# Second matrix of a feed-forward block by seven block products for 18 of 22 inner features, with two of four weight sums made in DRAM

## The chip, the core and the metric

The kernel runs on one core of a Trainium2 chip. The core has five engines that run side by side, each with its own instruction stream in order: TensorE (PE, matmuls; its weight loads are PEld), VectorE (DVE), ScalarE (ACT), GpSimd (POOL) and SyncE (SP, which here only issues DMA transfers). Sixteen DMA engines move data between DRAM and the on-chip memory SBUF; matmuls write into eight banks of PSUM. The metric is the time of one execution in microseconds (us).

## The reference

Two encoder layers over 544 tokens (512 of a first request, 32 of a later one). Each layer is a half-step feed-forward block (FFN), a mixer, and a second FFN, each with a residual and a LayerNorm. All numbers are float32.

```python
# x: 544 x 1024; D_MODEL = 1024, D_FF = 2816, ALPHA = 4 ** 0.25
def swiglu(x, w_in, w_out):
    gate, up = jnp.split(x @ w_in, 2, axis=-1)
    return (jax.nn.silu(gate) * up) @ w_out

x = layer_norm(ALPHA * x + 0.5 * swiglu(x, w_ffn_in[0], w_ffn_out[0]), ln_g[0], ln_b[0])
proj = x @ w_in                    # 1024 x 2560: pooling, convolution, attention inputs
...                                # mix = concat(pool, conv, attn) @ w_out
x = layer_norm(ALPHA * x + mix, ln_g[1], ln_b[1])
x = layer_norm(ALPHA * x + 0.5 * swiglu(x, w_ffn_in[1], w_ffn_out[1]), ln_g[2], ln_b[2])
```

## The kernel before, in words

**Layout.** Activations stand with channels on the 128 partitions and the 544 tokens along the row, in two halves of 272 (`HALF`). A model vector is `NK` = 8 tiles, the hidden vector `NF` = 22 tiles, called features. The residual stream is `y`, a view of `ya`.

**Splitting.** Every factor of a matmul is split into a high part (rounded, written by ACT) and a low part (the difference, by DVE). A product is then three matmuls: high weight by high data, low weight by high data, high weight by low data (`mm_h` L255, `mm_l` L259). A weight of 128x128 with a half of 272 tokens is the standard matmul here.

**Weights.** `Weights` holds a list of units in the order of use. SP loads a unit's raw blocks into the `raw` buffers; `part` makes the high (L172, ACT) and low (L173, DVE) parts in groups of up to 512 columns. A plain unit ("t") is one output column; a unit "s" holds four blocks of weights, from which `sums` makes four sums (L198, DVE) and seven groups. `get` lets the next unit's load and splitting be written one unit ahead of its matmuls, two for plain units.

**FFN.** `plan` walks over the 22 features. The first `NPLAIN` = 3 are computed plainly, the other 19 by seven products of blocks (`seven`, `hidden`): the token halves and the halves of the input channels form a 2x2 scheme, in which seven products replace eight. Their data sums come from `Blocks.add`. Each product goes through one PSUM bank and is taken out by ACT or DVE while the next runs (L341). The finished feature `sg` is split into `hh` and `hl`.

The second matrix runs in parts of `FSPLIT` = 8, 7, 7 features. As soon as one more feature than a part needs is done, each of its 8 output columns is computed plainly and added to `y` by DVE (`resid`, L449 and L451). The last part runs in `out_phase`, together with the LayerNorm.

**LayerNorm in `out_phase`.** After the second column a rough mean is subtracted (`shift`). For each further column DVE subtracts it (L377), ACT squares, and POOL adds to two accumulators (L380, L381); the columns that come last get the subtraction from POOL ahead of time (L388). For the last `nb` columns (2, in the program's last FFN 4) the two token halves run apart: all first halves, then all second halves, and DVE adds them to the accumulators (`add_last`, L393 to L396). `stats` (L405) sums the accumulators over the partitions on PE, `spread` (L419) copies the scale to all partitions, `scale` writes the next stage's data. PE runs remaining tail matmuls between these steps; a scheduler orders the instructions by priority.

Of the kernel before, what the change touches and what calls it, by code (L numbers as in the profile page):

```python
# [10 lines left out]
F32 = mybir.dt.float32  # L11
# [5 lines left out]
P = 128  # L17
# [13 lines left out]
FSPLIT = (8, 7, 7)  # L31
# [4 lines left out]
FB = 5  # L36
W_BUFS = 10
RAW_BUFS = 3
# [35 lines left out]
def encoder_kernel(  # L74
# [6 lines left out]
    w2: bass.AP,  # L81
    wi: bass.AP,
# [19 lines left out]
    xp = ctx.enter_context(tc.tile_pool(name="xp", bufs=34))  # L102
# [54 lines left out]
    class Weights:  # L157
# [24 lines left out]
        def load(self):  # L182
            kind, src, n = self.units[self.loaded]
            self.loaded += 1
            if kind == "t":
                raw = self.fetch()
                c = 0
                for part in src if isinstance(src, tuple) else (src,):
                    w = part.shape[-1]
                    nc.sync.dma_start(out=raw[:, c:c + w], in_=part)  # L190
                    c += w
                self.ready.append(Tile([self.group(raw[:, g:min(g + G, n)]) for g in range(0, n, G)]))
            else:
                self.ready.append(self.sums(src))

        def add(self, a, b):
            r = big["pool"].tile([P, G], F32, tag="sum", name="sum", bufs=4)
            V.tensor_tensor(out=r, in0=a, in1=b, op=ALU.add)  # L198
            return r

        def sums(self, src):

            raws = [self.fetch() for _ in range(2)]
            for i, raw in enumerate(raws):
                nc.sync.dma_start(out=raw, in_=src[:, 2 * i * G:2 * (i + 1) * G])
            b11, b12, b22, b21 = (raw[:, c:c + G] for raw in raws for c in (0, G))
            g11, g21 = self.group(b11), self.group(b21)
            r1 = self.add(b11, b12)
            r2 = self.add(r1, b22)
            g2, g1 = self.group(r2), self.group(r1)  # L210
            g3 = self.group(self.add(b12, b22))
            g22 = self.group(b22)
            return g11, g21, g2, g1, g3, g22, self.group(self.add(r2, b21))

        def first(self, x):

            units = self.units[:NSTART]
            raws = [self.fetch() for _ in units]
            tiles = [[self.new_group() for _ in range(2)] for _ in units]
            n = 2  # L220
            for i in range(NK // n):
                ks, cs = slice(n * i, n * i + n), slice(n * i * P, n * (i + 1) * P)
                nc.scalar.dma_start(out=ya[:, ks, HS[0]], in_=xT[:, ks, HS[0]])
                for raw, (_, src, _) in zip(raws, units):
                    o = slice(cs.start % G, cs.start % G + n * P)
                    nc.sync.dma_start(out=raw[:, cs], in_=src[cs.start // G][:, o])
            for i in range(NK // n):
                cs = slice(n * i * P, n * (i + 1) * P)
                o = slice(cs.start % G, cs.start % G + n * P)
                for k in range(n * i, n * i + n):  # L230
                    split(y[k], x[k], HS[0])
                for raw, groups in zip(raws, tiles):
                    hi, lo = groups[cs.start // G]
                    self.part(raw[:, cs], hi[:, o], lo[:, o])
# [17 lines left out]
    def mm_h(acc, w, x, k, h, first):  # L252

        for i, v in enumerate(w.at(k)):
            PE.matmul(acc[:, :HALF], v, x[k][0][:, HS[h]], start=first and i == 0, stop=False)  # L255

    def mm_l(acc, w, x, k, h, last):

        PE.matmul(acc[:, :HALF], w.at(k)[0], x[k][1][:, HS[h]], start=False, stop=last)  # L259
# [25 lines left out]
    def split(t, x, sl=slice(0, T), eng=None):  # L285
        hh, hl = x
        S.activation(out=hh[:, sl], in_=t[:, sl], func=AF.Copy)
        (eng or V).tensor_tensor(out=hl[:, sl], in0=t[:, sl], in1=hh[:, sl].bitcast(F32), op=ALU.subtract)
# [12 lines left out]
    def new_b(name):  # L301
# [852 lines left out]
```

## Time and profile before

| | |
|---|---|
| time, median of 3 runs | 2003.87 us (2002.77 to 2006.32) |
| profiled execution | 2006.03 us |
| its span | 2004.2 us |
| PE busy | 1973.7 us, 98% |
| DVE busy | 1449.9 us, 72% |
| ACT busy | 993.6 us, 50% |
| POOL busy | 225.6 us, 11% |
| moved on the load queue | 172.07 MB, 27.4% of the engines' time |

The busy shares are means over the whole span; a stage can be far from them. A matmul's printed duration overlaps the next one's, so the price of a matmul is the distance between starts. "Idle before <-releaser" names what ended an engine's idle time; an instruction without it followed the one before at once. The granted clock of PE was 0.99 of full speed.

### The profile page before, as it was taken

How to read it: one execution, taken by the hardware profiler on the slowest of the kernel's cores; microseconds unless marked ns; L12 is line 12 of the kernel's file. 1: busy time of each engine (PE TensorE's matmuls, PEld its weight loads, DVE VectorE, ACT ScalarE, POOL GpSimd, SP SyncE). 2: the span in 40 equal slices, each digit the busy share in tenths (PEclk: the TensorE clock that was granted, in tenths of full speed). 3: DMA queues.
4: the chain of work that ended last, by engine and by line, in shares of the span. 5: the costliest groups of instructions: out<-in, count | busy, mean ns of one | idle time of the engine just before them, and what ended most of it. 6: DMA issues, size and time to landing. Idle time of an engine off the chain costs nothing.

```text
span 2004.2 us, 38173 instructions
## 1 busy us (share of the span) xinstructions
PE 1973.7 (98%) x15446; PEld 1937.3 (97%) x15446; DVE 1449.9 (72%) x2806; ACT 993.6 (50%) x2000; POOL 225.6 (11%) x214
## 2 busy tenths in 40 slices
PE   9999999999999999999999999999999999999997
PEld 9999999999899999999999999999899999999997
DVE  7958677677658967768798496775865698576676
ACT  6625445465436544535466254454754366355453
POOL 0000000510134000000420000015001330000003
PEclk9999999999899999999999999999999999999999
DMA  6332323142121242323223223232421213323231
GB/s 208 113 102 95 99 83 116 64 144 92 59 81 63 87 123 67 116 85 102 89 73 108 85 93 109 85 106 72 140 98 54 85 50 99 106 85 109 89 98 46
DMA packets 65834, 189.12 MB, mean 94 GB/s; under 512 B 9428, under 2 KB 15188, under 8 KB 65656
## 3 DMA queue, kind: packets, MB, share of 16 engines
q1 hardware_dynamic: 55584, 172.07, 27.4%
q10 hardware_dynamic: 10072, 14.60, 2.3%
q8 instruction: 121, 1.98, 0.4%
q14 instruction: 57, 0.47, 0.1%
HBM read 179.88 MB, written 8.34 MB: 94 GB/s over the span
## 4 chain that ended last, share of the span: by engine, by line
PE 90%; DVE 6%; issue 1%; ACT 1%; DMA 1%; POOL 1%; POOLq 0%; ACTq 0%; DVEq 0%
PE b L341 39%; PE b L255 30%; PE b L259 15%; DVE wlo L173 1%; PE b L778 1%; PE b L777 1%; DVE sum L198 1%; PE b L793 1%; PE b L419 1%; DVE z L431 1%; ACT ya L433 1%; PE b L865 1%; PE b L758 0%; DMA raw<-in_w 0%; PE b L405 0%
## 5 line engine op out<-in xcount | busy, mean ns | idle before, releaser
L172 ACT ACTIVATE whi<-raw 128x512 fp32r<-128x512 f32 (+2 forms) x586 | 357.3, 614 | 495.6 <-PE b L259 299.1
L173 DVE TENSOR_TENSOR wlo<-raw,whi 128x512 fp32r<-128x512 f32 (+2 forms) x586 | 408.8, 700 | 149.0 <-ACT whi L172 144.2
L255 PE MATMUL b<-hh,wlo 128*128 128x272 f32 x1408 | 405.7, 288 | 0.0
L255 PE MATMUL b<-hh,whi 128*128 128x272 f32 x1408 | 405.1, 288 | 0.0
L259 PE MATMUL b<-hl,whi 128*128 128x272 f32 x1408 | 404.7, 287 | 0.0
L255 PE MATMUL b<-xh,whi 128*128 128x272 f32 x1024 | 296.3, 297 | 10.0 <-ACT xh L438 9.1
L172 ACT ACTIVATE whi<-sum 128x512 fp32r<-128x512 f32 x304 | 190.7, 631 | 201.4 <-PE b L259 99.5
L255 PE MATMUL b<-xh,wlo 128*128 128x272 f32 x1024 | 290.1, 290 | 0.1
L173 DVE TENSOR_TENSOR wlo<-sum,whi 128x512 fp32r<-128x512 f32 x304 | 207.8, 689 | 87.4 <-ACT whi L172 80.4
L259 PE MATMUL b<-xl,whi 128*128 128x272 f32 x1024 | 265.7, 290 | 0.0
L255 PEld LDWEIGHTS b<-hh,whi 128*128 128x128 f32 x1408 | 265.0, 188 | 0.0
L255 PEld LDWEIGHTS b<-hh,wlo 128*128 128x128 f32 x1408 | 264.9, 188 | 0.0
L259 PEld LDWEIGHTS b<-hl,whi 128*128 128x128 f32 x1408 | 264.9, 188 | 0.0
L341 PE MATMUL b<-xh,wlo 128*128 128x272 f32 x912 | 262.6, 288 | 0.0
L341 PE MATMUL b<-xh,whi 128*128 128x272 f32 x912 | 262.2, 288 | 0.0
L341 PE MATMUL b<-xl,whi 128*128 128x272 f32 x912 | 261.8, 287 | 0.0
L255 PEld LDWEIGHTS b<-xh,whi 128*128 128x128 f32 x1024 | 195.1, 191 | 14.0 <-ACT xh L438 11.7
L255 PEld LDWEIGHTS b<-xh,wlo 128*128 128x128 f32 x1024 | 195.5, 191 | 0.6 <-DVE wlo L173 0.3
L259 PEld LDWEIGHTS b<-xl,whi 128*128 128x128 f32 x1024 | 182.3, 190 | 0.7 <-issue 0.5
L341 PE MATMUL b<-s56h,whi 128*128 128x272 f32 x608 | 175.4, 289 | 3.3 <-ACT up L552 3.3
L388 POOL TENSOR_TENSOR ya<-ya,shift 128x544 f32<-128x544 f32 x14 | 25.3, 1830 | 1355.4 <-DVE wlo L173 1313.9
L341 PE MATMUL b<-s73h,wlo 128*128 128x272 f32 x608 | 175.3, 288 | 0.0
(208 smaller groups left out, 4248.1 us busy)
## 6 DMA issues: line engine op xcount, KB each, us to landing
raw<-in_w SPq DMA_DIRECT2D x184, 512.0 KB, 3.8
raw<-in_w SPq DMA_DIRECT2D x64, 448.0 KB, 3.3
raw<-in_wi SPq DMA_DIRECT2D x40, 512.0 KB, 3.2
raw<-in_w SPq DMA_DIRECT2D x42, 256.0 KB, 3.3
raw<-in_wo SPq DMA_DIRECT2D x16, 512.0 KB, 3.2
U<-scr ACTq DMA_DIRECT2D x8, 320.0 KB, 3.5
out_nkT<-k ACTq DMA_DIRECT2D x8, 272.0 KB, 2.1
out_nvT<-vT ACTq DMA_DIRECT2D x8, 272.0 KB, 2.2
```

What stands on the lines that cost most here:

```text
L172: S.activation(out=hi, in_=raw, func=AF.Copy)
L173: V.tensor_tensor(out=lo, in0=raw, in1=hi.bitcast(F32), op=ALU.subtract)
L198: V.tensor_tensor(out=r, in0=a, in1=b, op=ALU.add)
L255: PE.matmul(acc[:, :HALF], v, x[k][0][:, HS[h]], start=first and i == 0, stop=False)
L259: PE.matmul(acc[:, :HALF], w.at(k)[0], x[k][1][:, HS[h]], start=False, stop=last)
L341: PE.matmul(acc[:, :HALF], v[:, cs], x, start=opens and j == 0 and m == 0, stop=j == len(xs) - 1 and m == 2, skip_group_check=True)
L388: POOL.tensor_tensor(out=c, in0=c, in1=self.s, op=ALU.subtract)
L419: PE.matmul(b[:, c * CH:(c + 1) * CH], self.rstd[h][:, c:c + 1].to_broadcast([CH, P]), ident[:CH, :CH], start=True, stop=True)
L431: V.tensor_tensor(out=z, in0=c, in1=self.rstd[h], op=ALU.mult)
L433: S.activation(out=c, in_=z, func=AF.Identity, bias=b, scale=g)
L777: PE.matmul(g[:, :w], qc[c][parts[c], qs], kh[parts[c], :w], start=True, stop=False)
L778: PE.matmul(g[:, :w], qc[c][:, qs], kc[c][:, :w], start=False, stop=True)
```

## The change

The second matrix goes by the same seven products for the first 18 features, in three parts of six; the last four features stay plain and run with the LayerNorm. Features of a part go in pairs (even and odd), output columns in pairs too, so a part has four units of 63 matmuls (seven products of 3 pairs by 3), and its weights are four blocks of 384 columns. `resid7` adds each product to `y` straight from PSUM.

```diff
+    def resid7(m, alpha):
+        seen = set()
+        def step(i, h, op):
+            def f(acc):
+                c = y[m + i][:, HS[h]]
+                if alpha and (i, h) not in seen:
+                    V.scalar_tensor_tensor(out=c, in0=c, scalar=ALPHA, in1=acc, op0=ALU.mult, op1=op)
+                else:
+                    V.tensor_tensor(out=c, in0=c, in1=acc, op=op)
+                seen.add((i, h))
+            return f
+        add, sub = ALU.add, ALU.subtract
+        return [step(0, 0, add), step(0, 0, add), step(1, 0, sub), step(1, 1, add), step(1, 1, sub), step(1, 0, add),
+                step(0, 1, add)]
     def ffn(l, f, x, pre):
-        xb = Blocks(x)
-        hs = []
+        xb = Blocks(x[:NK // 2], x[NK // 2:])
+        last = len(FSPLIT) - 1
+        starts = [sum(FSPLIT[:s]) for s in range(last + 1)]
+        parts, tail = [], []
         for what, i in plan():
...
                 else:
                     sg = hidden(W.get(), xb)
-                hs.append(new_x("h"))
-                split(sg, hs[-1])
+                n = i - starts[last]
+                if n >= 0:
+                    tail.append(new_x("h") if n else new_b("h"))
+                    split(sg, tail[-1])
+                elif i % 2 == 0:
+                    if i in starts:
+                        parts.append(Blocks([], []))
+                    hb = parts[-1]
+                    hb.first.append(new_h("h", 1))
+                    split_half(sg, hb.first[-1], 0)
+                    held = sg
+                else:
+                    hb.second.append(new_x("h"))
+                    split(sg, hb.second[-1])
+                    hb.add(held, sg, new_x)
                 if i == 0:
                     W.ahead(3)
                 for k in range(2 * i, 2 * i + 2) if i < 2 else ():
-                    xb.add(y[k], y[k + NK // 2])
+                    xb.add(y[k], y[k + NK // 2], new_b)
                 continue
-            n = FSPLIT[i]
-            part, hs = hs[:n], hs[n:]
-            if i == len(FSPLIT) - 1:
-                return out_phase(l, 2 * f, part, range(n), False)
-            for m in range(NK):
-                acc = run(mm2(W.get(), part, range(n)))
-                for h in range(2):
-                    resid(m, acc[h], h, i == 0)
+            if i == last:
+                return out_phase(l, 2 * f, tail, range(FSPLIT[i]), False)
+            for m in range(0, NK, 2):
+                seven(W.get(), parts[i], resid7(m, i == 0))
```

The weight sums r1 and r3 of a unit "s" (all but the program's first two) come from DRAM: SP copies two blocks into one of eight DRAM tiles six units ahead, POOL's queue adds two others to it three units ahead, and the result is loaded like a raw block. DVE makes the sums r2 and r4.

```diff
+            self.sums_ahead()
             if kind == "t":
-                raw = self.fetch()
-                c = 0
-                for part in src if isinstance(src, tuple) else (src,):
-                    w = part.shape[-1]
-                    nc.sync.dma_start(out=raw[:, c:c + w], in_=part)
-                    c += w
-                self.ready.append(Tile([self.group(raw[:, g:min(g + G, n)]) for g in range(0, n, G)]))
+                parts = src if isinstance(src, tuple) else [src[:, g:min(g + G, n)] for g in range(0, n, G)]
+                self.ready.append(Tile([self.group(self.fetch(part)) for part in parts]))
             else:
-                self.ready.append(self.sums(src))
+                self.ready.append(self.seven(src, n, self.r13.pop(self.loaded - 1, None)))
+        def sums_ahead(self):
+            for ahead, todo, step in zip(SUMS_AHEAD, self.todo, (self.copy, self.accumulate)):
+                if todo and todo[0] < self.loaded + ahead:
+                    step(todo.pop(0))
+        def copy(self, i):
+            _, src, n = self.units[i]
+            if len(self.ring) < SUMS_AHEAD[0] + 2:
+                t = dram.tile([P, 2 * G], F32, name=f"r13_{len(self.ring)}")
+            else:
+                t = self.ring.pop(0)
+            self.ring.append(t)
+            self.r13[i] = t[:, :2 * n]
+            nc.sync.dma_start(out=self.r13[i], in_=src[:, :2 * n])
+        def accumulate(self, i):
+            _, src, n = self.units[i]
+            POOL.dma_start(out=self.r13[i], in_=src[:, n:3 * n], accum_op=ALU.add)
...
+        def seven(self, src, n, r13):
+            blocks = [src[:, :n], src[:, 3 * n:], src[:, 2 * n:3 * n]]
+            blocks += [src[:, n:2 * n]] if r13 is None else [r13[:, :n], r13[:, n:]]
+            b11, b21, b22, *b = (self.fetch(v) for v in blocks)
             g11, g21 = self.group(b11), self.group(b21)
-            r1 = self.add(b11, b12)
+            r1, r3 = b if b[1:] else (self.add(b11, b[0]), self.add(b[0], b22))
             r2 = self.add(r1, b22)
-            g2, g1 = self.group(r2), self.group(r1)
-            g3 = self.group(self.add(b12, b22))
-            g22 = self.group(b22)
+            g2, g1, g3, g22 = (self.group(v) for v in (r2, r1, r3, b22))
             return g11, g21, g2, g1, g3, g22, self.group(self.add(r2, b21))
```

Raw buffers are single blocks now, and other pools shrink.

```diff
 D_FF = 2816
 NF = D_FF // P
-FSPLIT = (8, 7, 7)
+FSPLIT = (6, 6, 6, 4)
 NPLAIN = 3
 NB = 2
 NSTART = 3
 AHEAD = 300
-FB = 5
+SUMS_AHEAD = (6, 3)
+SUMS_FROM = 2
+FB = 4
 W_BUFS = 10
-RAW_BUFS = 3
...
-        def fetch(self):
-            return wp.tile([P, 2 * G], F32, tag="raw", name="raw", bufs=RAW_BUFS)
+            self.r13, self.ring = {}, []
+            self.todo = [[i for i, u in enumerate(units) if u[0] == "s"][SUMS_FROM:] for _ in range(2)]
+        def fetch(self, src):
+            raw = wp.tile([P, G], F32, tag="raw", name="raw", bufs=RAW_BUFS)[:, :src.shape[-1]]
+            nc.sync.dma_start(out=raw, in_=src)
+            return raw
```

A feature's token halves can be tiles of their own, so that the half that is not needed isn't kept; `Blocks.add` serves hidden pairs too.

```diff
     def new_x(name):
-        return (xp.tile([P, T], F32R, tag="xs", name=f"{name}h"),
-                xp.tile([P, T], F32R, tag="xs", name=f"{name}l"))
...
+        return Feature(*(xp.tile([P, T], F32R, tag="xs", name=f"{name}{c}") for c in "hl"))
+    def new_b(name):
+        return Feature(*(big["pool"].tile([P, T], F32R, tag="xb", name=f"{name}{c}", bufs=XB) for c in "hl"))
+    def new_h(name, halves):
+        return Feature(*(tuple(xp.tile([P, HALF], F32R, tag="xh", name=f"{name}{c}", bufs=16) for _ in range(halves)) for c in "hl"))
+    def new_xs():
+        return [new_h("x", 2) if k < NK // 2 else new_x("x") for k in range(NK)]
...
+    def split_half(t, x, h):
+        S.activation(out=x.at(0, h), in_=t[:, HS[h]], func=AF.Copy)
+        V.tensor_tensor(out=x.at(1, h), in0=t[:, HS[h]], in1=x.at(0, h).bitcast(F32), op=ALU.subtract)
...
-        def __init__(self, plain):
-            self.plain, self.sums = plain, []
-        def add(self, e, o):
+        def __init__(self, first, second):
+            self.first, self.second, self.sums = first, second, []
+        def add(self, e, o, new):
...
-            s = [new_b(n) for n in ("s56", "s73")]
+            s = [new(n) for n in ("s56", "s73")]
```

The list of units:

```diff
@@ -1023,15 +1094,16 @@
                     if i < NPLAIN:
                         units += [("t", (src[:, a * G:(a + 1) * G], src[:, b * G:(b + 1) * G]), 2 * G) for a, b in ((0, 3), (1, 2))]
                     else:
-                        units.append(("s", src, 4 * G))
+                        units.append(("s", src, G))
+                elif i < len(FSPLIT) - 1:
+                    units += [("s", w2[l, f, i, q], FSPLIT[i] // 2 * P) for q in range(NK // 2)]
                 else:
-                    c0, n = sum(FSPLIT[:i]) * P, FSPLIT[i] * P
-                    units += [("t", w2[l, f, m, :, c0:c0 + n], n) for m in range(NK)]
+                    units += [("t", w2t[l, f, m], FSPLIT[i] * P) for m in range(NK)]
```

Not shown: the smaller calls that take a half of a feature by `at`, two loads that go to ACT's queue, and the order of the weights in DRAM.

**How the instructions move.** First PE in the first FFN's `out_phase`, around the statistics and the step that spreads the scale (`rstd` is the scale, `hh` and `hl` the last part's features, `xh` the next stage's data). Before:

```order
L259 MATMUL b<-hl,whi 128x272
L255 MATMUL b<-hh,whi 128x272
L255 MATMUL b<-hh,wlo 128x272
L259 MATMUL b<-hl,whi 128x272
L255 MATMUL b<-hh,whi 128x272
L255 MATMUL b<-hh,wlo 128x272
L259 MATMUL b<-hl,whi 128x272
L255 MATMUL b<-hh,whi 128x272
L419 MATMUL b<-ident,rstd 128x68 x4
L255 MATMUL b<-hh,wlo 128x272
L259 MATMUL b<-hl,whi 128x272
L255 MATMUL b<-hh,whi 128x272
L255 MATMUL b<-hh,wlo 128x272
```

Now:

```order
L276 MATMUL b<-hh,whi 128x272
L276 MATMUL b<-hh,wlo 128x272
L280 MATMUL b<-hl,whi 128x272
L276 MATMUL b<-hh,whi 128x272
L276 MATMUL b<-hh,wlo 128x272
L461 MATMUL b<-ident,rstd 128x68 x4
L280 MATMUL b<-hl,whi 128x272
L276 MATMUL b<-hh,whi 128x272
L276 MATMUL b<-hh,wlo 128x272
L280 MATMUL b<-hl,whi 128x272
L276 MATMUL b<-xh,whi 128x272
L276 MATMUL b<-xh,wlo 128x272
```

The scale is spread (L419, now L461) with 20 matmuls of the tail behind it before the next stage's first `xh` matmul, and now with 4; between the statistics and that step stand 13, now 11.

Next DVE. Before, in the second part of the second matrix, first FFN (`wlo` is a weight's low part, `ya` the residual, `sum` a weight sum, `b` a PSUM bank):

```order
L173 TENSOR_TENSOR wlo<-sum,whi 128x512 [waits Activation_49]
L451 TENSOR_TENSOR ya<-ya,b 128x272 [waits PE_49]
L198 TENSOR_TENSOR sum<-raw 128x512 [waits DMAHW4_49,DVE_49]
L173 TENSOR_TENSOR wlo<-sum,whi 128x512 [waits Activation_49]
L198 TENSOR_TENSOR sum<-sum,raw 128x512 [waits DMAHW5_49,DVE_49]
L451 TENSOR_TENSOR ya<-ya,b 128x272 [waits PE_49]
L173 TENSOR_TENSOR wlo<-sum,whi 128x512 [waits Activation_49]
L451 TENSOR_TENSOR ya<-ya,b 128x272 [waits PE_49]
L198 TENSOR_TENSOR sum<-raw 128x512 [waits DVE_49]
```

Now, in the same part:

```order
L183 TENSOR_TENSOR wlo<-raw,whi 128x384 [waits Activation_49]
L224 TENSOR_TENSOR sum<-raw 128x384 [waits DMAHW7_49,DMAHW6_49]
L634 TENSOR_TENSOR ya<-ya,b 128x272 [waits DVE_49,PE_49]
L183 TENSOR_TENSOR wlo<-raw,whi 128x384 [waits DMAHW2_49,Activation_49]
L634 TENSOR_TENSOR ya<-ya,b 128x272 [waits PE_49]
L183 TENSOR_TENSOR wlo<-raw,whi 128x384 [waits Activation_49]
L224 TENSOR_TENSOR sum<-sum,raw 128x384 [waits DMAHW4_49,DVE_49]
L634 TENSOR_TENSOR ya<-ya,b 128x272 [waits PE_49]
L183 TENSOR_TENSOR wlo<-sum,whi 128x384 [waits Activation_49]
L634 TENSOR_TENSOR ya<-ya,b 128x272 [waits DVE_49,PE_49]
L183 TENSOR_TENSOR wlo<-raw,whi 128x384 [waits DMAHW3_49,Activation_49]
L634 TENSOR_TENSOR ya<-ya,b 128x272 [waits PE_49]
```

There was one addition to `ya` for 21 matmuls. Now there is one for each product of nine, behind one low part, or a low part and a sum.

Last SP, where the second matrix's weights are loaded. Before, in the first FFN:

```order
L190 DMA raw<-in_w 128x1024 [waits DMAHW1_49,DVE_49,Activation_49]
L190 DMA raw<-in_w 128x1024 [waits DMAHW2_49,DVE_49,Activation_49]
L190 DMA raw<-in_w 128x1024 [waits DMAHW3_49,DVE_49]
L190 DMA raw<-in_w 128x1024 [waits DMAHW4_49,DVE_49]
L190 DMA raw<-in_w 128x1024 [waits DMAHW5_49,DVE_49]
L190 DMA raw<-in_w 128x1024 [waits DMAHW6_49,DVE_49]
```

Now (`r_3` to `r_5` are DRAM tiles):

```order
L175 DMA raw<-in_w 128x384 [waits DVE_49,Activation_49]
L175 DMA raw<-in_w 128x384 [waits DVE_49]
L216 DMA r_3_589<-in_w 128x1024 [waits DMAHW6_49,DMAHW5_49,DMAHW1_49]
L175 DMA raw<-in_w 128x384 [waits DMAHW2_49,DVE_49]
L175 DMA raw<-r_4_745 128x384 [waits DMAHW3_49,DMASW4_49,DVE_49]
L175 DMA raw<-r_4_745 128x384 [waits DMAHW4_49,DVE_49]
L175 DMA raw<-in_w 128x384 [waits DVE_49]
L216 DMA r_4_745<-in_w 128x1024 [waits DMAHW4_49,DMAHW3_49]
L175 DMA raw<-in_w 128x384 [waits DMAHW7_49,DVE_49]
```

A load waited only for its buffer. Now a copy of 1024 columns stands among the loads, and it waits for earlier transfers, the reads of its own tile among them.

## Rows read from the trace of the kernel before

**Rows 1.** The page's first part: the span, and busy time of each engine:

```profile
span 2004.2 us, 38173 instructions
PE 1973.7 (98%) x15446; PEld 1937.3 (97%) x15446; DVE 1449.9 (72%) x2806; ACT 993.6 (50%) x2000; POOL 225.6 (11%) x214
```

**Rows 2.** Timeline of PE: start, duration, engine, line, operation, tiles, count [idle before <-releaser]:

```profile
329.76 0.29 PE L341 MATMUL b<-s56l,whi 128*128 128x272 f32 x1
...
335.14 0.29 PE L255 MATMUL b<-hh,whi 128*128 128x272 f32 x1
```

**Rows 3.** Windows: stretch, length, busy (instructions) of PE, PEld, DVE, ACT, POOL; PEclk, DMA, GB/s:

```profile
125.00:150.00 25.00, 25.00 (x202) 25.00 (x201) 12.38 (x22) 5.67 (x9) 0.00 (x0) 1.00 0.22 69
175.00:200.00 25.00, 25.00 (x202) 25.00 (x201) 22.88 (x42) 15.77 (x29) 0.00 (x0) 1.00 0.38 120
660.00:670.00 10.00, 8.74 (x70) 8.52 (x69) 9.69 (x17) 5.32 (x11) 0.00 (x0) 1.00 0.38 117
1956.00:1976.00 20.00, 20.00 (x162) 20.00 (x161) 15.07 (x21) 5.77 (x12) 16.00 (x10) 1.00 0.00 1
1977.89:1991.38 13.49, 12.24 (x102) 11.68 (x101) 10.83 (x30) 6.16 (x13) 1.01 (x1) 1.00 0.18 63
15.00:20.00 5.00, 5.00 (x42) 5.00 (x41) 2.86 (x10) 2.53 (x7) 0.00 (x0) 1.00 0.97 328
```

**Rows 4.** Waits of PE: line, releaser, us in total, times, longest:

```profile
PE b L341 <- ACT up L552: 3.3, 3, 1.3
```

**Rows 5.** Timeline of DVE in the first FFN, by seven products and in the last part:

```profile
189.71 0.72 DVE L288 TENSOR_TENSOR hl<-sg,hh 128x544 fp32r<-128x544 f32 x1
190.35 0.68 DVE L198 TENSOR_TENSOR sum<-raw 128x512 f32<-128x512 f32 x1
190.95 0.68 DVE L173 TENSOR_TENSOR wlo<-sum,whi 128x512 fp32r<-128x512 f32 x1
191.55 0.43 DVE L564 TENSOR_TENSOR up<-b,up 128x272 f32<-128x272 f32 x1
191.90 0.68 DVE L198 TENSOR_TENSOR sum<-sum,raw 128x512 f32<-128x512 f32 x1
...
341.15 0.56 DVE L173 TENSOR_TENSOR wlo<-raw,whi 128x384 fp32r<-128x384 f32 x1
```

**Rows 6.** Timeline of POOL in the first LayerNorm:

```profile
347.00 3.72 POOL L388 TENSOR_TENSOR ya<-ya,shift 128x544 f32<-128x544 f32 x2 [346.56 <-DVE wlo L173]
...
352.01 1.83 POOL L381 TENSOR_TENSOR acc<-acc,sq 128x544 f32<-128x544 f32 x1
...
370.20 1.37 POOL L381 TENSOR_TENSOR acc<-acc,sq 128x544 f32<-128x544 f32 x1
```

**Rows 7.** Timeline of DVE beside POOL:

```profile
350.85 1.77 DVE L173 TENSOR_TENSOR wlo<-raw,whi 128x512 fp32r<-128x512 f32 x1 [1.02 <-ACT whi L172]
```

**Rows 8.** Timeline of PE in the first LayerNorm:

```profile
373.32 0.38 PE L405 MATMUL b<-onesd,acc 128*68 128x1 f32 x4
...
382.68 0.40 PE L255 MATMUL b<-xh,whi 128*128 128x272 f32 x1 [2.11 <-ACT xh L438]
```

**Rows 9.** Timeline of POOL in the last LayerNorm:

```profile
1956.75 5.04 POOL L388 TENSOR_TENSOR ya<-ya,shift 128x544 f32<-128x544 f32 x3 [322.79 <-DVE wlo L173]
```

**Rows 10.** Timeline of DVE in the last LayerNorm:

```profile
1973.78 0.44 DVE L395 TENSOR_TENSOR acc<-acc,ya 128x272 f32<-128x272 f32 x1
...
1975.13 0.44 DVE L395 TENSOR_TENSOR acc<-acc,ya 128x272 f32<-128x272 f32 x1
```

**Rows 11.** Timeline of PE in the last LayerNorm:

```profile
1977.89 0.62 PE L405 MATMUL b<-onesd,acc 128*68 128x1 f32 x8
...
1991.38 0.65 PE L405 MATMUL b<-onesd,acc 128*68 128x1 f32 x8 [1.01 <-DVE acc L395]
```

**Rows 12.** The page's DMA parts: a queue, and issues of one kind:

```profile
q1 hardware_dynamic: 55584, 172.07, 27.4%
...
raw<-in_w SPq DMA_DIRECT2D x42, 256.0 KB, 3.3
```

More of the change, by code (lines that the diff above doesn't have):

```diff
@@ L196, in add @@
+        def accumulate(self, i):
+            _, src, n = self.units[i]
+            POOL.dma_start(out=self.r13[i], in_=src[:, n:3 * n], accum_op=ALU.add)
         def add(self, a, b):
-            r = big["pool"].tile([P, G], F32, tag="sum", name="sum", bufs=4)
+            r = big["pool"].tile([P, G], F32, tag="sum", name="sum", bufs=3)[:, :a.shape[-1]]
             V.tensor_tensor(out=r, in0=a, in1=b, op=ALU.add)
             return r
[L201 to L206, printed above, removed]
+        def seven(self, src, n, r13):
+            blocks = [src[:, :n], src[:, 3 * n:], src[:, 2 * n:3 * n]]
+            blocks += [src[:, n:2 * n]] if r13 is None else [r13[:, :n], r13[:, n:]]
+            b11, b21, b22, *b = (self.fetch(v) for v in blocks)
@@ L254, in mm_h @@
         for i, v in enumerate(w.at(k)):
-            PE.matmul(acc[:, :HALF], v, x[k][0][:, HS[h]], start=first and i == 0, stop=False)
+            PE.matmul(acc[:, :HALF], v, x[k].at(0, h), start=first and i == 0, stop=False)
     def mm_l(acc, w, x, k, h, last):
-        PE.matmul(acc[:, :HALF], w.at(k)[0], x[k][1][:, HS[h]], start=False, stop=last)
+        PE.matmul(acc[:, :HALF], w.at(k)[0], x[k].at(1, h), start=False, stop=last)
     def mm(acc, w, x, ks, h):
@@ L325, in products @@
         def products(self):
-            e, o = self.plain[:NK // 2], self.plain[NK // 2:]
+            e, o = self.first, self.second
             s56, s73 = ([s[i] for s in self.sums] for i in range(2))
             for xs, h in ((e, 0), (o, 0), (s56, 1), (s56, 0), (s73, 0), (s73, 1), (o, 1)):
-                yield [tuple(v[:, HS[h]] for v in x) for x in xs]
+                yield [(x.at(0, h), x.at(1, h)) for x in xs]
     def seven(ws, blocks, after):
@@ L436, in scale @@
                 return
-            xh, xl = self.x[k]
-            S.activation(out=xh[:, sl], in_=c, func=AF.Copy)
-            POOL.tensor_tensor(out=xl[:, sl], in0=c, in1=xh[:, sl].bitcast(F32), op=ALU.subtract)
+            xh, xl = (self.x[k].at(i, h) for i in range(2))
+            S.activation(out=xh, in_=c, func=AF.Copy)
+            POOL.tensor_tensor(out=xl, in0=c, in1=xh.bitcast(F32), op=ALU.subtract)
         def apply(self, h, k):
@@ L491, in out_phase @@
         if not ln.final:
-            ln.x = [new_x("x") for _ in range(NK)]
+            ln.x = new_xs()
         g = tail_mm(1, 1)
@@ L1033, in encoder_kernel @@
     W = Weights(units)
-    x = [new_x("x") for _ in range(NK)]
+    x = new_xs()
     warm = bank()
@@ L1041, in encoder_kernel @@
     nc.sync.dma_start(out=cnt, in_=c_cnt)
-    pre = start(x, lambda h, k: split(y[k], x[k], HS[h]), {}, NK)
+    pre = start(x, lambda h, k: split_half(y[k], x[k], h), {}, NK)
     for l in range(DEPTH):
@@ L1083, in _blocks @@
 def _blocks(a):
[L1085 to L1087 removed]
+    b = np.stack([a[..., c, :, r, :, :] for r, c in ((0, 0), (0, 1), (1, 1), (1, 0))], axis=-3)
+    return b.reshape(*b.shape[:-3], -1)
 def kernel(**inputs):
```

50 lines of the change are left out of this document (27 added, 23 removed).

## The prediction

> **What bounds the kernel now.** I read the page's busy shares first. TensorE (PE) is busy 1973.7 us of a span of 2004.2, VectorE (DVE) 1449.9 [rows 1]. So a matmul that disappears is worth its own length, unless something that PE's work covers today comes into sight. Next the timeline of PE, for the price: between the first and the last row of [rows 2] lie 43 matmuls of 272 columns in 5.38 us, 0.1251 us each. (Their printed 0.29 us overlap one another; the spacing is the price.) Then the windows of three stages, for the cover (the first three of [rows 3]). In the second matrix (125 to 150 us) DVE works 12.38 of 25 us, in the first one by seven products (175 to 200) 22.88 of 25, and where an FFN begins (660 to 670) 9.69 of 10 while PE drops to 8.74. The reader is to see that the stage that gets shorter has half of DVE free, and that the stage ahead of it has hardly any. PE's waits on a product's bank [rows 4] and the price of DVE's pieces [rows 5] come next, and last the LayerNorm at the end of an FFN: GpSimd (POOL) [rows 6], DVE beside it [rows 7], PE behind it [rows 8], and the same in the program's last FFN [rows 9 to 11]; the transfers are [rows 12].
>
> The profiled execution took 2006.03 us, 1.83 around its span; the median shown is 2003.87. Terms come from that execution, and I subtract their sum from the median (from 2006.03 it would come out 2.2 later).
>
> **Matmuls removed.** Per FFN 18 of 22 features go from 8 x 18 x 2 x 3 = 864 matmuls to 12 units of 63, 756. That is 108 less, 432 in four FFNs: 432 x 0.1251 = **54.0 us**, all on the path. A unit of the second matrix lasts 63 x 0.1251 = 7.88 us, one of its products 1.13 us.
>
> **DVE in the second matrix.** A piece costs its spacing on the timeline [rows 5]: 512 columns 0.60 (190.35 to 190.95 us), 544 columns 0.64, 272 columns 0.35; for 384 columns, printed at 0.56, I take 0.48, in proportion. A unit now asks for 7 low parts and 2 sums of 384 and 7 additions out of PSUM: 9 x 0.48 + 7 x 0.35 = 6.8 of 7.88 us, 86%, where the stage had half of its time free [rows 3]. It fits, so I charge no bulk. But a product's bank comes round again two products later (the code's order of banks), so an addition must start within some 0.4 us (1.13, less 0.29 for the last matmul to end and 0.43 for the addition). One low part and one sum ahead of it make 0.96. PE's waits of this kind come to 3.3 us over the 76 units of the first matrix today [rows 4]; at worst I allow 0.3 us in each of 48 units. Ends 0 and 14, and I take **4**, near the row.
>
> **DVE in the first matrix.** A unit had 11 pieces of 512 (7 low parts, 4 sums), five of 272 and one of 544: 9.0 us of 10.5. Two sums of 512 go, and every second feature gets the sums of its pair (four of 272, two low parts of 544; the even one's split is halved). The average stays 9.0, with 10.6 in odd and 7.5 in even features, which the queue of weights ahead evens out. I charge nothing. Where an FFN begins DVE is the bound; up to two pairs fall in there, 2 x 2.7 us less the sums saved. Ends 0 and 7 over four FFNs, I take **2**.
>
> **The LayerNorm loses its cover.** This is the large term. The last part is 4 plain features, so a column of the output takes 24 matmuls, 3.0 us, where it took 42, 5.25. POOL's chain keeps its length. It starts when the second column is done and the shift subtracted: today 10.5 + 1.36 us into the phase (the phase starts at 335.14 [rows 2], POOL at 347.00 [rows 6]), then 6.0 + 1.4 = 7.4. It runs 3.7 us of subtractions and five pairs of additions at 3.0 to 3.7 (1.37 to 1.83 an addition), so it ends at 26.4 to 29.5. The statistics follow 1.7 later (POOL ends at 371.57, they start at 373.32 [rows 6, 8]): 28.1 to 31.2. PE is there after 18.0 + 3.0 + 1.5 = 22.5 and waits 5.6 or more; I take the low end, POOL's pace of today. Behind the statistics 15 tail matmuls now cover the way to the first matmul of the next stage, not 33; the 2.11 us wait there today [rows 8] grows by 18 x 0.125 = 2.2. That is 7.8 per FFN, with ends 5.0 (every POOL operation at its shortest, 1.37: 7.4 + 2.7 + 13.6 + 1.7 - 22.5 + 2.2) and 10.9.
> The last FFN has four columns in its tail. POOL starts 11.9 us into the phase, at 1956.75 [rows 9], and works 16.0 us (the window from 1956 in [rows 3]); four rounds of additions follow on DVE at 1.35 us [rows 10], the first of them beside POOL's last, and end 4.7 after POOL. Then the statistics come at 7.4 + 16.0 + 4.7 = 28.1, where PE arrives at 19.5; today they come 33.0 us into the phase, at 1977.89 [rows 11]. From there to the second half's statistics PE took 13.5 us [rows 11], of which DVE worked 10.83 [rows 3]; that doesn't shrink, so I put 11.5. 33.0 + 13.5 becomes 28.1 + 11.5: 6.9 gained in a phase that loses 144 matmuls, 18.0 us. So 11.1 is lost (ends 8.5, with POOL at 1.37 an operation, and 13). Together 3 x 7.8 + 11.1 = **34.5**, ends 23 and 46; were only the cover behind the statistics lost, 3 x 2.2 + 8 = 15.
> The phase's first matmuls need the last hidden feature after 9 matmuls, 1.1 us, where they had 2.3; its product and its difference alone take 0.43 and 0.64 [rows 5], with a copy between. I take **1.5** over four FFNs (0 to 4).
>
> **Transfers.** Each unit adds a copy (SyncE, SP) and an accumulation (POOL), DRAM to DRAM, neither of which this trace shows. Bounds from loads: the 16 engines move 328 GB/s at a share of 0.97 (the last of [rows 3]) and 172.07 MB in 27.4% of the span is 313 [rows 12]; I take 318. A unit of the second matrix moves 0.98 MB of loads, 0.52 of copy and 0.46 of accumulation in 7.88 us, 250 GB/s if each byte counts once, 308 if the accumulation counts twice (it also reads its target), 375 if both do. The first matrix needs 212, 256 or 300. Only the last case of the second matrix is above 318.
> SP is a queue: the copy for a later unit waits until the reads of its ring tile, issued just before, have landed, and the next loads stand behind it. Seven raw buffers for five loads give 7/5 x 7.88 = 11.0 us for one turn: the wait (a latency), the load's own landing (another) and 0.5 for the last reader. It holds while a load lands within 5.3 us; 256 KB take 3.3 today [rows 12]. POOL's accumulation waits for a copy issued three units, over 20 us, earlier; what stands behind it there has no work to lose. I charge 0 here. At the start, the engines are full already (0.97, [rows 3]), and the first ring tiles add 1 MB or so: **2** (0 to 4).
> ScalarE gains 7 copies of 384 per unit and has half of its time free [rows 1]: nothing.
>
> **Sum.** -54.0 + 34.5 + 1.5 + 4 + 2 + 2 = -10: **1994 us**.
>
> **Rivals.**
> *The LayerNorm costs its lower end* (POOL, less disturbed by DVE, keeps 1.37 an addition, like the last row of [rows 6]): 23 in place of 34.5, and the small terms at half: -26, 1978. For it: both lengths stand in one chain. Against: DVE is denser now, and [rows 7] shows a low part of 1.77 us beside POOL, 0.68 without [rows 5]; they hinder each other.
> *The small waits eat the rest*: 46 for the LayerNorm, or 14 for PSUM beside 34.5: 0 to +2, 2004 to 2006, about no change. For it: DVE at 86%, every addition behind a low part. Against: the first matrix runs at 22.88 of 25 today with hardly a wait of PE [rows 3, 4].
> *Slower: the transfers become the bound of the second matrix.* Place: 12 stages of four units. It decides at a landing of 5.3 us, or when copy and accumulation both count double: (375/318 - 1) x 7.88 x 48 = 67 us more, 2061. For it: 512 KB copies between the loads lengthen each landing, and SP waits for landings. Against: a stage lasts only 31 us, and the ring is filled six units ahead.
> The DMA engines' share would rise from 0.22 in such a stage [rows 3]. The Trainium skill, DMA: Bandwidth & Descriptors, section "Issuing engines are not separate DMA queues", says that transfers started by different engines end up on the same 16 engines and interleave. By that rule POOL's accumulations delay SP's loads; if they only had a path of their own, this rival would fall to the 250 GB/s case and to nothing.
> *Slower: POOL's transfers hold DVE up.* 122 accumulations, each built by POOL, which is idle in these stages today. If each stops DVE as an addition of POOL does (1.1 more in [rows 7], up to 1.8 in [rows 6]), a unit of the second matrix needs 8.2 of 7.88 us and an odd one of the first 12.0 of 10.5: 17 us there and up to 55 here, 45 in all, 2039. It decides from 1.0 us each. Against: no row shows POOL building a transfer.
> The row of 1.77 us is DVE reading two operands beside POOL's addition. The Trainium skill, SBUF — State Buffer, section "Who interferes with whom", says that a DVE instruction with two SBUF inputs contends only with a GpSimd instruction that reads SBUF, not with one that only writes it. By that rule the building of a transfer, if it only writes, costs DVE nothing, and this rival falls away; no run here shows it yet.
>
> **How the numbers follow.** About 0.2%, 4 us, can be told from no change. Forecast 0.43 (0.38 faster, 0.04 the same, 0.01 slower; its own range 1981 to 2005). LayerNorm at its lower end 0.22, all faster. Small waits 0.15 (0.03, 0.08, 0.04). Transfers 0.12 and POOL's transfers 0.08, both slower. Together 0.63 faster, 0.12 the same, 0.25 slower. The range leaves out the two slower rivals, 0.2: at the bottom -54 + 15 and nothing else, 1965; at the top all terms at their worst would be -54 + 75 = +21; they do not all come at once, so I stop at +15, 2019.
>
> **What would show it.** Right: a pitch of 7.9 us per unit of the second matrix with PE at 100%; a wait of PE for the accumulated sums of 5 to 8 us in each of three LayerNorms, and 8 in the last; the wait for the first xh at 4 us or more; copies landing in under 5 us. Wrong: waits of PE for weights in the second matrix with a DMA behind them (transfers); low parts of 1.8 us beside accumulations (POOL's transfers); no wait at the statistics (then the time is below 1980).

## The result, and the profile after

The changed kernel takes 2159.94 us, median of 4 runs (2158.85 to 2168.42), against 2005.09 of the kernel before: ratio 1.0783, 95% interval 1.0753 to 1.0813. I had forecast 1994, within 1965 to 2019. The matmuls that were to go are gone, and 208 us of other time came in their place.

First the page of the changed kernel: its span, busy times, two DMA queues, and issues (KB each, median us from issue to landing). They answer to [rows 1, 12].

```profile
span 2158.1 us, 40276 instructions
...
PE 1997.9 (93%) x15014; PEld 1943.2 (90%) x15014; DVE 1640.0 (76%) x3354; ACT 1108.0 (51%) x2248; POOL 330.8 (15%) x336
...
q1 hardware_dynamic: 139008, 258.51, 39.0%
q0 software_dynamic: 17568, 57.68, 17.3%
...
raw<-in_w SPq DMA_DIRECT2D x272, 256.0 KB, 4.5
r<-in_w SPq DMA_DIRECT2D x74, 512.0 KB, 5.3
r<-in_w POOLq DMA_DIRECT2D x74, 512.0 KB, 6.2
raw<-r SPq DMA_DIRECT2D x148, 256.0 KB, 4.3
```

PE has 432 instructions fewer and is busy for 24 us longer. The reader should stop there: fewer matmuls take longer in sum. The granted clock, as a mean over the execution, is 0.96, and it was 0.99. The accumulations (q0) move 57.68 MB in 17.3% of 2158.1 us: 154 GB/s of the 16 engines, where loads reach about 313 [rows 12]. A load of 256 KB lands in 4.5 us, not 3.3, and a copy in 5.3.

Next the waits of PE, DVE and SP (who waits <- for whom: us in total, times, longest).

```profile
PE b L383 <- DVE ya L634: 53.2, 28, 4.3
PE b L447 <- DVE acc L437: 33.0, 7, 7.2
PE b L383 <- DVE ya L632: 22.2, 12, 4.1
...
DVE sum L224 <- DMA raw<-r: 154.5, 76, 4.9
...
SPq L216 <- DMA raw<-r: 170.3, 73, 5.3
```

Read alone, the first row says that PE waits for DVE to empty a bank, so DVE would be too dense. The fourth says more: DVE itself stands for 154.5 us, at a weight sum of a later unit whose input, a load from DRAM, has not landed. The timeline of one such stop shows the two together (SP, DVE, then PE).

```profile
102.49 0.89 SPq L175 DMA_DIRECT2D raw<-r  x2
...
105.79 0.56 DVE L183 TENSOR_TENSOR wlo<-raw,whi 128x384 fp32r<-128x384 f32 x1
109.47 0.56 DVE L224 TENSOR_TENSOR sum<-raw 128x384 f32<-128x384 f32 x1 [3.12 <-DMA raw<-r]
109.94 0.43 DVE L632 SCALAR_TENSOR_TENSOR ya<-ya,b 128x272 f32<-128x272 f32 x1
...
110.76 0.78 DVE L634 TENSOR_TENSOR ya<-ya,b 128x272 f32<-128x272 f32 x2
...
111.25 0.59 PE L383 MATMUL b<-hh,whi 128*128 128x272 f32 x1 [2.91 <-DVE ya L634]
111.64 0.43 PE L383 MATMUL b<-hh,wlo 128*128 128x272 f32 x1
```

The load is issued at 102.5 and lands at about 109.4. DVE, in order, waits 3.1 us for it with two additions out of PSUM behind it; PE has no bank and stops for 2.9 us; its matmuls then come 0.23 us apart. The windows show what that is (stretch, length, PE, PEld, DVE, ACT, POOL busy, granted clock, DMA share, GB/s): the restart, a whole stage of the second matrix, one of the first, the LayerNorm's wait, and the program's last stage of the second matrix.

```profile
111.20:115.20 4.00, 3.95 (x19) 3.95 (x20) 2.77 (x7) 0.98 (x2) 0.00 (x0) 0.57 0.93 201
99.00:141.00 42.00, 36.04 (x258) 35.29 (x256) 31.85 (x69) 16.17 (x30) 4.06 (x5) 0.92 0.83 206
141.00:206.00 65.00, 63.02 (x502) 62.58 (x501) 54.17 (x108) 40.25 (x77) 4.87 (x6) 1.00 0.83 203
418.00:424.00 6.00, 3.21 (x20) 2.90 (x21) 3.51 (x7) 0.60 (x2) 1.17 (x1) 0.53 0.00 0
...
2036.11:2070.30 34.19, 32.60 (x254) 31.88 (x253) 30.38 (x65) 16.24 (x29) 0.00 (x0) 1.00 0.45 136
```

After the stop PE has a granted clock of 0.57, near the lower of its two levels (1.2 of 2.4 GHz). The stage's 252 matmuls should take 31.5 us and take 41.6; the DMA engines are busy for 0.83 of the time, where they were at 0.22 [rows 3]. The last row is a control inside the same kernel: in this stage no copy and no accumulation is left to issue, VectorE does the work of any other such stage, and the stage takes 34.2 us, where the eleven others take 38 to 44.5.

The account, by spans (2004.2 and 2158.1). A stage's excess is its length less its matmuls at 0.1251 us.

| us | forecast | measured |
|---|---|---|
| matmuls removed | -54.0 | -54.0 |
| excess of the 12 stages of the second matrix | 4 | 114 (76 of it PE idle, the rest slower matmuls) |
| excess of the first matrix by blocks | 0 | 32 (37, less 5 before) |
| LayerNorm phases, net of their matmuls | 36 | 48 (33 in three, 15 in the last) |
| the rest: start of the program, mixers, starts of the FFNs | 4 | 14 |
| sum | -10 | +154 |

### The profile page after: what moved, and what is told of

Its sections match the earlier page's. It is cut to its first block, busy times and chain, and to the rows that moved or that the text cites. A ratio compares the mean times of both kernels' runs of the same rounds, so it can differ in the third digit from the quotient of the medians.

```text
span 2158.1 us, 40276 instructions
## 1 busy us (share of the span) xinstructions
PE 1997.9 (93%) x15014; PEld 1943.2 (90%) x15014; DVE 1640.0 (76%) x3354; ACT 1108.0 (51%) x2248; POOL 330.8 (15%) x336
## 3 DMA queue, kind: packets, MB, share of 16 engines
q0 software_dynamic: 17568, 57.68, 17.3%
## 4 chain that ended last, share of the span: by engine, by line
PE 61%; DVE 15%; DMA 14%; issue 6%; ACT 2%; POOL 2%; DVEq 0%; SPq 0%; ACTq 0%; POOLq 0%
PE b L383 35%; PE b L276 13%; DMA raw<-r 12%; PE b L280 7%; DVE wlo L183 6%; DVE sum L224 2%; ACT whi L182 1%; PE b L849 1%; PE b L848 1%; DVE ya L634 1%; DMA raw<-in_w 1%; PE b L864 1%; POOL acc L422 1%; DVE s L358 1%; DVE z L473 1%
## 5 line engine op out<-in xcount | busy, mean ns | idle before, releaser
L182 ACT ACTIVATE whi<-raw 128x512 fp32r<-128x512 f32 (+2 forms) x814 | 481.1, 595 | 562.6 <-PE b L383 430.3
L183 DVE TENSOR_TENSOR wlo<-raw,whi 128x512 fp32r<-128x512 f32 (+2 forms) x814 | 542.6, 674 | 86.3 <-ACT whi L182 74.3
L383 PE MATMUL b<-s73h,whi 128*128 128x272 f32 x896 | 271.3, 303 | 72.6 <-DVE ya L634 49.8
L220 POOL DMA_DIRECT2D r<-in_w x122 | 99.5, 816 | 1191.5 <-DMA r<-in_w 1131.3
L383 PE MATMUL b<-s73l,whi 128*128 128x272 f32 x896 | 266.5, 297 | 0.0
L383 PE MATMUL b<-s56h,wlo 128*128 128x272 f32 x896 | 258.7, 289 | 0.0
L383 PE MATMUL b<-s56l,whi 128*128 128x272 f32 x896 | 258.5, 289 | 0.0
L383 PEld LDWEIGHTS b<-s73h,whi 128*128 128x128 f32 x896 | 176.6, 197 | 82.6 <-DVE ya L634 29.8
L276 PEld LDWEIGHTS b<-xh,whi 128*128 128x128 f32 x1024 | 199.5, 195 | 18.0 <-ACT xh L480 12.0
L182 ACT ACTIVATE whi<-sum 128x512 fp32r<-128x512 f32 (+1 forms) x252 | 148.3, 589 | 125.7 <-PE b L383 94.3
L224 DVE TENSOR_TENSOR sum<-raw 128x512 f32<-128x512 f32 (+1 forms) x126 | 80.2, 638 | 154.8 <-DMA raw<-r 154.5
L383 PEld LDWEIGHTS b<-xh,whi 128*128 128x128 f32 x912 | 173.8, 191 | 20.3 <-DVE sg L609 19.1
```

What stands on the lines that cost most here:

```text
L182: S.activation(out=hi, in_=raw, func=AF.Copy)
L183: V.tensor_tensor(out=lo, in0=raw, in1=hi.bitcast(F32), op=ALU.subtract)
L220: POOL.dma_start(out=self.r13[i], in_=src[:, n:3 * n], accum_op=ALU.add)
L276: PE.matmul(acc[:, :HALF], v, x[k].at(0, h), start=first and i == 0, stop=False)
L383: PE.matmul(acc[:, :HALF], v[:, cs], x, start=opens and j == 0 and m == 0, stop=j == len(xs) - 1 and m == 2, skip_group_check=True)
```

## The experiments

Theories of the 114 + 32: **A**, copies and accumulations load the 16 engines so that loads land late; **B**, SP stands at each copy and the loads behind it start late; **C**, DVE is too dense.

**No transfers in DRAM.**

```diff
-            self.r13[i] = t[:, :2 * n]
-            nc.sync.dma_start(out=self.r13[i], in_=src[:, :2 * n])
+            self.r13[i] = src[:, n:3 * n]
...
-            POOL.dma_start(out=self.r13[i], in_=src[:, n:3 * n], accum_op=ALU.add)
+            pass
```

> Leaves out the copies and the accumulations: the two blocks that were read from the DRAM tiles are read from the weights' own place (so r1 and r3 are not the sums). Loads, buffers, vector work and matmuls stay. Theory A (the 16 engines are so full of copies and accumulations that the loads land late) and theory B (SyncE stands at each copy until the reads of its tile have landed, and the loads behind it start late) both expect the excess of the seven-product stages (114 us in the second matrix, 37 in the first, beside 63 resp. 84 matmuls at 0.125 us) to go: 2005 to 2015 us. Theory C (VectorE at 87% is too dense, and the additions out of PSUM stand behind low parts and sums whatever the transfers do) expects at most 30 us of it: 2130 or more.

Measured 2037.43 us, ratio 1.015 (1.0135 to 1.0165). The stages' excess falls from 151 to 34 us: it was the transfers. The landings of the loads (the last line of the view of line 175, SP's loads) show it too, first for the stage from 99 to 141 us of the changed kernel, then for the same stage here, 90 to 124:

```profile
DMA to landing us min/median/max: 2.8/5.0/7.5
```

```profile
DMA to landing us min/median/max: 2.2/3.3/3.8
```

C is out as the main cause. The expectation's upper end was 22 us too low, since 34 us of the excess stay.

**No accumulations.** The second half of that edit alone.

> Leaves out the accumulations only (r1 and r3 stay the copied blocks). The copies stay on SyncE with their waits. Theory A: the accumulations are 17 of the 58 points of the engines' share, landings fall to some 3.5 us, so most of the excess goes: 2015 to 2040 us. Theory B: SyncE still waits at every copy for the reads of its tile, so at most a third goes: 2110 or more. Theory C: 2130 or more.

Measured 2058.69 us, ratio 1.0256 (1.0235 to 1.0277), excess 59. The copies, with SP's waits for them, cost 21 us, the accumulations 101. This speaks for A; the time lies between the two expectations, nearer to A's.

**Copies from POOL.**

```diff
-            nc.sync.dma_start(out=self.r13[i], in_=src[:, :2 * n])
+            POOL.dma_start(out=self.r13[i], in_=src[:, :2 * n])
```

> The copies are issued from GpSimd's queue, ahead of the accumulations, so SyncE waits for buffers only; bytes and number of transfers stay. Theory B: the 170 us that SyncE stood at copies are gone and loads start earlier: 2020 to 2050 us. Theory A: the engines carry the same: 2140 or more. Theory C: 2130 or more.

Measured 2158.5 us, ratio 1.0756 (1.0738 to 1.0774). That is A's value, but two things cancel in it. The excess fell by 33 us, to 118, and the first block product begins at 75.5 us, where it began at 52.1. If the new queue changed nothing else in these stages, SP's waits are about a fifth of the excess; the start is 23 us later with it.

**All sums on DVE.**

```diff
-SUMS_FROM = 2
+SUMS_FROM = 999
```

> All four sums on VectorE, none in DRAM: four loads for a unit, no copies, no accumulations; VectorE gets two more sums per unit (1.2 us in the first matrix, 0.96 in the second: 10.3 of 10.5 us and 7.8 of 7.9). Theories A and B: the transfers' excess goes, the denser VectorE gives back some 20 to 50 us: 2025 to 2060. Theory C: slower than with the sums in DRAM, 2170 or more.

Measured 2022.49 us, ratio 1.0078 (1.0062 to 1.0094): better than every version with sums in DRAM. A window over a stage of the second matrix (PE, PEld, DVE, ACT, POOL):

```profile
92.50:123.50 31.00, 30.64 (x240) 30.07 (x239) 30.55 (x71) 13.67 (x30) 0.00 (x0) 1.00 0.40 114
```

And two of PE's waits:

```profile
PE b L447 <- DVE acc L437: 31.5, 7, 7.1
...
PE b L383 <- DVE ya L632: 0.4, 1, 0.4
```

DVE is busy for 30.55 of 31.00 us, and PE waits for an addition to empty its bank once in the whole program, 0.4 us. The stages' excess is 20 us. A dense DVE by itself costs next to nothing here; one that waits costs a lot. C is refuted.

**Plain copies for accumulations**, one or two.

```diff
-            POOL.dma_start(out=self.r13[i], in_=src[:, n:3 * n], accum_op=ALU.add)
+            POOL.dma_start(out=self.r13[i], in_=src[:, n:3 * n])
```

> Each accumulation becomes a plain copy of the same bytes on the same queue, with the same waits (so r1 and r3 are not the sums). Theory A (bytes through the 16 engines; an accumulation costs them twice a load's time per byte): half of the 101 us between leaving the accumulations out (2059) and having them (2160): 2090 to 2125 us. Theory D (the accumulating itself is slow, or its result comes late): 2060 to 2080.

> Each accumulation becomes two plain copies of the same bytes, one after the other, on the same queue. Theory A: the same engine time as an accumulation, so the time of the changed kernel: 2140 to 2180 us. Theory D: as with one copy, 2060 to 2085.

Measured 2082.34 us with one (ratio 1.0394, 1.0377 to 1.0412) and 2210.54 with two (1.1032, 1.1016 to 1.1049). POOL's queue in the first and in the second:

```profile
q0 software_dynamic: 14496, 57.68, 9.3%
```

```profile
q0 software_dynamic: 28992, 115.36, 17.4%
```

Two plain copies take the engine time of an accumulation (17.4% and 17.3%) and cost more than it does, so the adding is not what hurts. Nor does its result come late: in the changed kernel SP stands for 1.9 us in all at loads whose DRAM tile isn't finished. D is refuted. Over the run with the copies alone, one plain copy takes half of that time and costs 24 us, two cost 152: the cost rises much faster than the load. Both values lie outside A's ranges, which were drawn as a straight line (the first 8 us below, the second 31 above).

**Six raw buffers** in the kernel without the transfers (`RAW_BUFS = 6`).

> As the kernel that left copies and accumulations out (2037 us; so r1 and r3 are not the sums), with 6 raw buffers in place of 7 for the five loads of a unit. If what a late landing costs is set by how soon a buffer comes round again (7/5 of a unit, 11.0 us, against 9.5 with six), fewer buffers cost as slower landings did: 2060 to 2110 us. If landings alone count (2.4 to 3.3 us there, the same now): 2033 to 2042.

Measured 2032.96 us, ratio 1.0144 (1.0127 to 1.0161), as with seven. The turn of the buffers, on which my bound of 5.3 us rested, doesn't bind while loads land in time.

**Another order of loads** in the changed kernel.

```diff
-            b11, b21, b22, *b = (self.fetch(v) for v in blocks)
+            b11, b22, *b = (self.fetch(v) for v in blocks[:1] + blocks[2:3] + blocks[1:2] + blocks[3:])
+            b22, b[0] = b[0], b22
+            b21 = self.fetch(src[:, 3 * n:])
```

> The changed kernel with another order of a unit's five loads: r1 second and b21 last, in place of fourth and second, so that the first sum that VectorE makes (r1 + b22) has its inputs two loads earlier. Same bytes. If the only harm is that this one load lands late: 2060 to 2100 us (against 2160). If the engines' load makes every load late, whichever comes last is waited for: 2130 or more.

Measured 2360.12 us, ratio 1.1738 (1.1695 to 1.1782), 200 worse. DVE's and SP's largest waits for a transfer:

```profile
DVE sum L224 <- DMA raw<-in_w: 321.3, 131, 7.3
...
SPq L216 <- DMA raw<-r: 404.6, 109, 8.1
```

Over half of DVE's waiting (169 us) is at the sum that takes the last load, b21, which mostly stands right behind a copy at which SP waits (in 74 of 122 cases); the rest is at the first sum, now for b22. Whatever comes last is late, as A expects; and B's mechanism, about a fifth of the loss in the changed kernel, grows to 404.6 us of waiting when the load that DVE needs stands behind it.

**The LayerNorm alone**: the kernel before, its second matrix all plain, with the changed kernel's parts.

```diff
-FSPLIT = (8, 7, 7)
+FSPLIT = (6, 6, 6, 4)
```

> The kernel before, with its second matrix in plain parts of 6, 6, 6 and 4 features: the same matmuls, none by blocks in the second matrix, no transfers added; only the LayerNorm runs beside 24 matmuls per column in place of 42. Theory E (the LayerNorm's loss is the lost cover alone, 11 us in each of three and 15 in the last): 48 us more, 2045 to 2060. Theory F (it comes from the denser VectorE of the block products): within 12 us of before, 2000 to 2018.

Measured 2066.43 us, ratio 1.0308 (1.0293 to 1.0323), with one of the waits behind it:

```profile
PE b L405 <- DVE acc L395: 30.8, 7, 7.1
```

With the same matmuls as before and no block product in the second matrix, the new parts cost 62 us, more than the 54 that the change removes; 51 of them lie in the four LayerNorm phases (each has 144 matmuls fewer, 18.0 us, and got only 2.5 to 6.5 us shorter). The first FFN's phase takes 41.1 us from its first matmul to the next stage, like 41.0 in the changed kernel (47.5 before). E holds, and its size was too small.

**Ten features in the tail**, sums on DVE.

```diff
-FSPLIT = (6, 6, 6, 4)
+FSPLIT = (6, 6, 10)
-SUMS_FROM = 2
+SUMS_FROM = 999
```

> All sums on VectorE, and the second matrix by seven products for 12 of 22 features, in parts of 6 and 6; the last 10 stay plain beside the LayerNorm. 72 matmuls fewer per FFN than before, 288 x 0.125 = 36 us; a column of the output takes 60 matmuls, 7.5 us, so the LayerNorm is covered better than before. With some 3 us lost per FFN to the denser VectorE: 1975 to 1990 us. If VectorE (10.3 of 10.5 us per unit of the first matrix) or the LayerNorm ate it: 2000 or more.

Measured 1987.78 us, ratio 0.9917 (0.9903 to 0.9932). PE's wait for the accumulated sums is 2.5 us in all. It beats the kernel before.

**The same with the first matrix's sums in DRAM.**

```diff
-[i for i, u in enumerate(units) if u[0] == "s"][SUMS_FROM:]
+[i for i, u in enumerate(units) if u[0] == "s" and u[2] == G][SUMS_FROM:]
```

> The kernel with the last 10 features plain (1988 us), with the sums r1 and r3 of the first matrix made in DRAM again and those of the second on VectorE. Theory A: a unit of the first matrix moves 2.9 MB in 10.5 us if an accumulation counts twice, 275 of some 318 GB/s; most of its loads have time, so 1990 to 2025 us, no gain. If the sums in DRAM relieve VectorE enough to matter: 1972 to 1982.

Measured 2056.47 us, ratio 1.0275 (1.0232 to 1.0317): 69 worse than without, beyond both ranges. The profiled execution took 2073.93, 17 above the median. Two windows over such stages, and DVE's wait for a load:

```profile
125.00:190.00 65.00, 61.63 (x478) 61.11 (x477) 56.86 (x116) 36.11 (x69) 4.06 (x5) 0.97 0.77 204
...
260.00:300.00 40.00, 36.62 (x271) 36.19 (x270) 26.86 (x49) 21.17 (x39) 3.25 (x4) 0.91 0.80 205
```

```profile
DVE sum L224 <- DMA raw<-r: 105.5, 40, 12.3
```

The engines are busy for 0.77 and 0.80 of the time; had the 478 and 271 matmuls come at 0.1251 us each, the same work would have made 0.84 and 0.94. That is below what I took as their limit, and DVE stands 105.5 us at sums of loads that haven't landed (12.3 of them in one stop). So a loss doesn't need the limit to be reached.

**Three columns in the last tail.**

```diff
-        nb = 2 * NB if ln.final else NB
+        nb = 3 if ln.final else NB
...
-            for i in range(2, nb):
-                g = tail_mm(i, 1)
-                steps(g, 3)
-                for k in range(3 * i - 4, min(3 * i - 1, NK)):
-                    ln.apply(0, k)
-                run(g)
+            g = tail_mm(2, 1)
+            for k in range(2, NK):
+                steps(g, 1)
+                ln.apply(0, k)
+            run(g)
```

> The kernel with the last 10 features plain, with three columns in place of four in the tail of the last FFN. Four tails of three groups are more than the ten weight groups; with three, the last FFN's end should lose less: 1978 to 1986 us against 1988. If the groups don't matter: 1986 to 1994.

Measured 1980.5 us, ratio 0.9876 (0.9861 to 0.9891), the best version. With three columns the scaling of the first half has to be spread over the third column's matmuls, so the edit is two things at once; which of them gains the 7 us stays open.

## Why the prediction was wrong

*Matmuls.* Right: 432 fewer, 54 us.

*Transfers.* This is the step that failed: "I charge 0 here". Its middle case, an accumulation counting twice, was right (154 against some 300 GB/s), and gave 308 of 318 GB/s, 0.97 of the limit. I took a stage below the limit for free. By the engines' time these stages stood at it: the 12 stages keep the engines busy for 385 us (share times length), and their matmuls take 378. And the cost begins long before. Over the run without transfers it is 21 us with the copies (251 us of engine time in these stages), 45 with one plain copy more (316), 123 with the accumulation (385), 173 with two copies (398). A mean rate is no test where each load must land in time and an in-order engine stands behind it. My other test, a landing of 5.3 us, was passed by the median (4.3 to 4.6) while the stage lost a quarter. It was not passed by every load: of the loads that SP issued in these stages and whose landing the trace has, 38 of 205 took longer, and none of 203 without the transfers. It also counted the turn of the buffers, and what bound was DVE at the sum; the sign that I had named, PE waiting for weights, didn't come, since PE was stopped at its banks.

*The rival "transfers"* named the place, the sign and SP's part in it, with a chance of 0.12; its price, 67 us, was little more than half of the measured 151 less 34, since it priced only bytes above the limit, and left out the clock: 38 of the 114 us are not idle time but matmuls further apart, about 25 of them in stretches at the lower clock, as after the stop above.

*DVE in the second matrix.* I charged 4 us for additions behind low parts. In the changed kernel PE does wait for such additions, 75 us, and with all sums on DVE and no such transfers, at a denser DVE, 0.4. The density by itself costs next to nothing; the wait in the queue does.

*The rival "POOL's transfers hold DVE up"* fell (its price, 45 us, was also less than its two terms, 17 and up to 55, without a reason). POOL builds an accumulation for 0.81 us, and DVE's sum beside it takes its usual time:

```profile
117.26 0.81 POOL L220 DMA_DIRECT2D r<-in_w  x1 [7.55 <-DMA r<-in_w]
...
117.87 0.56 DVE L224 TENSOR_TENSOR sum<-raw 128x384 f32<-128x384 f32 x1 [0.75 <-DMA raw<-r]
```

This sum has two SBUF inputs. So have the 128 sums and low parts of 384 columns that run beside the building of an accumulation; none takes more than 0.56 us. The Trainium skill, SBUF — State Buffer, section "Who interferes with whom", says that a DVE instruction with two SBUF inputs contends with a GpSimd instruction that reads SBUF, not with one that only writes it. The trace agrees if the building only writes, which no run here shows.

*The LayerNorm.* The mechanism was right, the term 34.5 + 1.5 came out at 48. The first one, against [rows 6, 8]:

```profile
398.59 3.75 POOL L430 TENSOR_TENSOR ya<-ya,shift 128x544 f32<-128x544 f32 x2 [28.77 <-ACT shift L413]
402.29 1.86 POOL L422 TENSOR_TENSOR acc<-ya 128x544 f32<-128x544 f32 x1
...
417.85 1.32 POOL L423 TENSOR_TENSOR acc<-acc,sq 128x544 f32<-128x544 f32 x1
...
420.79 0.36 PE L447 MATMUL b<-onesd,acc 128*68 128x1 f32 x2 [7.11 <-DVE acc L437]
...
431.75 0.59 PE L276 MATMUL b<-xh,whi 128*128 128x272 f32 x1 [2.69 <-ACT xh L480]
```

PE waits 7.1 us, where I said 5.6 or more: eight of ten additions take 1.8 us, the upper end. I had taken the mean of a chain with gaps in it; once POOL is the bound there are no gaps. That the longer additions are those beside DVE is likely by [rows 5, 7], and was not tested by itself. The last wait is 2.7 and not 4.3, but after the stop PE runs at a clock of about 0.5 (418 to 424 above), and it takes 11.0 us from the statistics to the next stage, with 15 tail matmuls between them, where it took 9.4 with 33. The mixer's and the FFN's start behind it lose some of the 14 us in the account's last line too.

*What stays open.* The split between late landings and SP's waits is known only roughly (a fifth for SP, from a run in which the start changed as well); a ring of more DRAM tiles, which would have taken SP's waits away and left the rest, was not tried. Nor was it tried whether more raw buffers in the changed kernel would have hidden the late landings: six in place of seven were tested only without the transfers. Why the first matrix's sums alone cost 69 us at shares of 0.77 and 0.80 was not tested further.

## What to carry to other kernels

Don't test an added transfer against the engines' rate alone: ask which in-order engine first touches what it brings, and what stands behind that instruction; here a late load stopped a vector sum, the sum held up the additions out of PSUM, and they stopped PE and its clock. Where PE waits for a vector engine, look at what that engine waits for before calling it too busy; at 99% busy it was no bound here. And a stage that gets shorter must still cover what ran beside it: pick the part that stays plain by the length of the chain that it covers.

## What the hardware showed that I had not expected

An accumulation from DRAM to DRAM takes about twice the engine time of a plain copy per byte (154 against 300 GB/s, the two-copy run's 115.36 MB in 17.4% of 2209.3 us). Cost grew far faster than load: +24 us for a first plain copy's 9.3%, +128 for the second's 8.1. A stop of PE of 2.9 us was followed by matmuls 0.23 us apart at a granted clock of 0.57; in the second matrix a third of the loss is matmuls further apart, not idle time.
